# A decoder step on one core: front steps in another order, twelve more gathers ahead of a fence, and the last 32 keys' scores as three float32r products

## The chip, the core and the metric

The kernel runs on one core of a Trainium2 chip, in one launch. A core has five engines that run side by side, each with a queue of its own in fixed order: TensorE (PE in the profile; its weight loads are listed as PEld), VectorE (DVE), ScalarE (ACT), GpSimd (POOL) and SyncE (SP). SP, ScalarE and GpSimd also issue transfers, which share 16 DMA engines. The metric is the device time of one execution in microseconds (us).

## The reference, cut to what matters

512 prompt tokens and 8 x 4 sample tokens (544 in all) of width 1024 pass one layer. The first half mixes tokens: a projection to six parts, retention over chunks of 128 tokens in four heads, a causal convolution of width 31 with a norm, an output projection and a norm. The second half picks experts: 8 heads find 16 of 16384 experts for each token from two lists of 128 keys.

```python
q = (xb @ w_query).reshape(PEER_BLOCK, PEER_HEADS, PEER_DQ)
s1 = jnp.einsum('phd,hkd->phk', q1, sub_keys_1)
...
idx = e1 * N_KEYS + e2
gate = jax.nn.softmax(sv.astype(jnp.float32), axis=-1)
u = jnp.take(peer_u, idx, axis=0)
act = jax.nn.gelu(jnp.einsum('phkd,pd->phk', u, xb), approximate=False)
vv = jnp.take(peer_v, idx, axis=0)
return jnp.einsum('phk,phkd->pd', gate * act, vv)
```

The result is added to the scaled token and normalised again. All of it is float32.

## The kernel before, in words

The tokens are split into groups. Group 0 (prompt tokens 0 to 127) passes the first half alone, early. The rest (416 tokens: 32 samples, then three chunks of 128 prompt tokens) follows. Two ways lead through the experts:

- **Gathers** (`gather`, L567) for group 0, for group "s" (the samples; four lanes of 32, so 32 slots) and for group "b" (the first 128 of the later prompt tokens; 128 slots). A slot is one indirect transfer of 1 MB (L572, from GpSimd: one row of `u` and `v` for each of 128 tokens), a dot product on VectorE (L575), GELU and weight on ScalarE (L579, L580) and an addition to `acc` on VectorE (L585). The tiles come from pool `gp`, three buffers, with one more for every fourth slot (`gx` in the front for group 0, `gx2` for group "b").
- **The dense way** for the last 256 tokens (`ND`): all 128 x 128 experts are computed. For each of 128 table rows ("keys" `e` in the code), `scores_of` (L778) loads 512 KB of `u` and makes eight products of 128 x 128 by 256 columns in float32; GELU is taken and multiplied by the gates; `v_stage` (L914) loads 512 KB of `v` and adds four products of 512 columns to four PSUM banks `pB`, which hold two blocks of 128 tokens. The gate weights are built from comparisons (`build`, L855: ScalarE `off` and `A`, VectorE `M` and `B`, bf16 products on TensorE) for eight tokens at a time. `first_keys` (L888) builds keys 0 to 95, `last_keys` (L907) keys 96 to 127.

The keys lie in four groups (`EG`, `E0S`): 0 to 31 in `GW[0]`, 32 to 51 in `GW[1]`, 52 to 95 in `GW[2]`, 96 to 127 in `GW[3]`. Scores of groups 2 and 0 are made first (L830, L835), those of group 1 inside `first_keys`, and those of group 3 in `phases` (L923), one to each value row, once `last_keys` has ended. In `phases`, pool `gb` (group 0) is closed after its 32 value rows and `gd` (group 3) opened in its place.

The order of the work: each engine's queue follows a planner, which simulates the program at build time and takes the earliest instruction in program order that it holds to be ready. `behind` adds an order without a wait. One such order is the **fence** (L576): the dots of group "b" and those of group "s" from slot `FREE` (12) on come behind the last instruction of `first_keys` on VectorE. `run` (L597, L965) traces one value row and two gather slots in turn.

The front around the change (L690 to L750): the GLU projection, the convolution (`conv`), the value projection, `rope` for q and for k (L696, L697), retention of chunks 1 and 2 (L711, L712), the gate projection (`silu_gate`, L714), loads of `w_out` (L715), the sample columns' copies (L716, L718), the convolution's norm (`conv_norm`, L717), `gate_heads` for chunks 1 and 2, retention of chunk 3 (L741), `gate_heads` for it, and then the output projection and norm of four parts in turn (`mix_a`, `mix_b`, L743 to L750). Weights come through pool `wp`, four buffers of 1 MB, loaded from SP. Behind it (L797 to L804) the queries of the expert half are projected for two heads at a time over all 416 columns, and the top 16 are found (`retrieve`, L510).

At the end (L966 on) the two blocks of `pB` are normalised in turn into tiles of pool `uvp` and stored.

Of the kernel before, what the change touches and what calls it, by code (L numbers as in the profile page):

```python
# [8 lines left out]
F32 = mybir.dt.float32  # L9
F32R = mybir.dt.float32r  # L10
# [9 lines left out]
D = 1024  # L20
# [14 lines left out]
UV = 4  # L35
FREE = 12
# [57 lines left out]
def tile_step(ctx: ExitStack, tc: tile.TileContext, a, o):  # L94
# [50 lines left out]
    def load_win(blk):  # L145
        return load_w(a["w_in"], blk * 512)
# [631 lines left out]
    def scores_of(e):  # L778

        u = uvp.tile([128, D], F32, name="uv").rearrange("p (k e) -> p k e", k=8)  # L780
        nc.sync.dma_start(u, a["ut"][e])
        sp = pdn.tile([128, ND], F32, name="sp")
        for k in range(8):
            T.matmul(sp, u[:, k], x1T[:, k, NG2:], start=(k == 0), stop=(k == 7))  # L784
        return sp
# [45 lines left out]
    gbs = ExitStack()  # L831
    gb = gbs.enter_context(tc.tile_pool(name="gb", bufs=1, side="right", reuse_waits="tile"))
# [10 lines left out]
    gc = ctx.enter_context(tc.tile_pool(name="gc", bufs=1, reuse_waits="tile"))  # L843
# [70 lines left out]
    def v_stage(e):  # L914
        vt = uvp.tile([128, D], F32, name="uv")
        nc.sync.dma_start(vt, a["uv"][e * NK:(e + 1) * NK, D:])
        W = place(e)
        for b in range(2):
            for q in range(2):
                T.matmul(pB[b][q], W[:, b * 128:(b + 1) * 128], vt[:, q * 512:(q + 1) * 512],  # L920
                         start=False, stop=(e == NK - 1), skip_group_check=True)

    def phases():  # L923
        for e in range(EG[0]):
            v_stage(e)
            yield
        gbs.close()
        gd = ctx.enter_context(tc.tile_pool(name="gd", bufs=1, side="right", reuse_waits="tile"))
        GW[3] = gd.tile([128, EG[3], ND], F32, name="Gd")
        b = last_keys()  # L930
        more = iter(range(E0S[3], NK))
        for e in range(E0S[1], E0S[3]):
            v_stage(e)
            if next(b, "end") == "end":
                for _ in range(1):
                    k = next(more, None)
                    if k is not None:
                        s_stage(k)
            yield
        for e in range(E0S[3], NK):  # L940
            v_stage(e)
            yield

# [74 lines left out]
```

## Time and profile before

| what | value |
| --- | --- |
| device time, three runs | 1611.17, 1598.4, 1602.21 us; median 1602.21 |
| profiled execution, its own time | 1603.19 us |
| its span, first to last instruction | 1601.4 us |
| mean granted TensorE clock | 0.971 |
| busy PE, DVE, ACT, POOL | 1494.5, 1225.3, 604.3, 374.1 us |
| transfers | 503.75 MB, 315 GB/s over the span |

The page gives busy time in 40 slices as digits of a tenth. A line of a stretch of the span gives its bounds and length, then busy time and count of each engine, the granted TensorE clock, the DMA engines' busy share and GB/s. A waiting line reads: who waited, for whom, us in total, times, longest. A line of the timeline reads: start, length, engine, line of the kernel, operation, out<-in, shapes, count, and in brackets the idle time before it and what ended it. A busy TensorE is not TensorE at its peak, since matmuls overlap and their ends are modelled; starts of successive groups are safer.

### The profile page before, as it was taken

What the parts mean: (1) busy time and instruction counts of PE and PEld (TensorE: products, weight loads), DVE (VectorE), ACT (ScalarE), POOL (GpSimd) and SP (SyncE); (2) the same over time, 40 slices, a digit from 0 to 9 for tenths busy, and PEclk for the clock granted to TensorE, in tenths of its full rate; (3) what the DMA queues carried; (4) which work ended last, traced back from release to release, by engine and by line L of the source; (5) the groups of instructions that cost most, each with busy time, mean ns of one, the idle gap of its engine ahead of it and who ended that gap; (6) DMA issues with size and microseconds to landing.
All of it is one profiled execution on the core that took longest, in us unless ns stands there. A gap on an engine that the chain in (4) does not pass through costs nothing.

```text
span 1601.4 us, 20802 instructions
## 1 busy us (share of the span) xinstructions
PE 1494.5 (93%) x7014; PEld 1010.1 (63%) x7014; DVE 1225.3 (77%) x3158; ACT 604.3 (38%) x1687; POOL 374.1 (23%) x335
## 2 busy tenths in 40 slices
PE   6899999996979999999999997999999999999996
PEld 6788556564756667788788875444566655543332
DVE  3939989989865999999852788566777777766666
ACT  2235542254222323333623888413994111111111
POOL 1001423444321222321120000122223222222221
PEclk9899999998989999999999997999999999999998
DMA  9458778997698669997794321998999999999995
GB/s 355 180 195 347 253 280 301 354 364 253 253 383 321 260 250 340 345 340 271 251 413 157 108 86 57 398 402 332 385 365 380 423 424 424 424 423 424 424 424 211
DMA packets 99543, 503.75 MB, mean 315 GB/s; under 512 B 10183, under 2 KB 21191, under 8 KB 56549
## 3 DMA queue, kind: packets, MB, share of 16 engines
q0 software_dynamic: 42240, 305.12, 48.7%
q1 hardware_dynamic: 50749, 189.96, 31.3%
q10 hardware_dynamic: 6448, 7.36, 1.5%
q8 instruction: 55, 0.90, 0.2%
q14 instruction: 51, 0.42, 0.1%
HBM read 497.03 MB, written 5.80 MB: 314 GB/s over the span
## 4 chain that ended last, share of the span: by engine, by line
PE 32%; DMA 28%; DVE 24%; issue 8%; ACT 4%; POOL 2%; SPq 0%; DVEq 0%; POOLq 0%; ACTq 0%
DMA g<-in_uv_dram,Ib 17%; PE pB L920 10%; PE sp L784 9%; PE mm L198 7%; DMA g<-in_uv_dram,I 7%; DVE acc L585 6%; DVE g L575 4%; POOL g L572 2%; ACT off L862 2%; PE mm L875 2%; PE mm L308 2%; DMA g<-in_w_in_dram 2%; DMA uv<-in_uv_dram 1%; DVE iu L504 1%; DVE score L505 1%
## 5 line engine op out<-in xcount | busy, mean ns | idle before, releaser
L784 PE MATMUL sp<-x1T,uv 128*128 128x256 f32 x2048 | 464.7, 384 | 15.4 <-ACT Ga L830 9.4
L784 PEld LDWEIGHTS sp<-x1T,uv 128*128 128x128 f32 x2048 | 385.5, 191 | 89.5 <-issue 23.2
L585 DVE SCALAR_TENSOR_TENSOR acc<-g,wgt,acc 128x1024 f32<-128x1024 f32 x285 | 365.0, 1281 | 99.3 <-ACT wgt L580 98.1
L572 POOL DMA_INDIRECT g<-in_uv_dram,I x128 | 181.9, 1421 | 435.1 <-DVE acc L585 222.6
L579 ACT ACTIVATE act<-act 128x1 f32<-128x1 f32 x288 | 57.9, 201 | 592.4 <-DVE g L575 592.0
L575 DVE SCALAR_TENSOR_TENSOR g<-g,x1g 128x1024 f32<-128x1024 f32 x160 | 195.3, 1224 | 94.2 <-DMA g<-in_uv_dram,Ib 63.1
L572 POOL DMA_INDIRECT g<-in_uv_dram,Ib x128 | 133.5, 1043 | 517.9 <-DVE acc L585 318.5
L575 DVE SCALAR_TENSOR_TENSOR g<-g,x 128x1024 f32<-128x1024 f32 x128 | 155.6, 1217 | 31.9 <-DMA g<-in_uv_dram,I 31.8
L198 PE MATMUL mm<-x1T,w 128*128 128x384 f32 (+1 forms) x512 | 176.1, 500 | 0.2 <-ACT score L524 0.2
L920 PE MATMUL pB<-uv,Ga 128*128 128x512 f32 x352 | 162.1, 604 | 1.1 <-DMA uv<-in_uv_dram 0.8
L862 ACT ACTIVATE off<-row,e1T 128x128 bf16<-128x128 bf16 x512 | 157.8, 388 | 1.5 <-PE mm L875 0.4
L198 PEld LDWEIGHTS mm<-x1T,w 128*128 128x128 f32 x512 | 96.6, 190 | 71.4 <-issue 37.9
L920 PE MATMUL pB<-uv,Gd 128*128 128x512 f32 x256 | 117.2, 601 | 2.1 <-DMA uv<-in_uv_dram 1.0
L920 PE MATMUL pB<-uv,Gb 128*128 128x512 f32 x256 | 115.4, 604 | 2.9 <-DMA uv<-in_uv_dram 2.5
L920 PEld LDWEIGHTS pB<-uv,Ga 128*128 128x128 f32 x352 | 63.7, 189 | 83.7 <-issue 63.1
L920 PEld LDWEIGHTS pB<-uv,Gd 128*128 128x128 f32 x256 | 46.1, 189 | 73.3 <-issue 48.2
L875 PEld LDWEIGHTS <-A 128*128 128x128 bf16 x1536 | 64.6, 100 | 36.6 <-issue 32.0
L920 PEld LDWEIGHTS pB<-uv,Gb 128*128 128x128 f32 x256 | 48.1, 193 | 59.6 <-issue 54.3
L875 PE MATMUL mm<-B,A 128*128 128x96 bf16 (+1 forms) x1536 | 68.4, 197 | 13.3 <-DVE Gc L901 12.4
L864 ACT ACTIVATE A<-off 128x1024 bf16<-128x1024 bf16 x64 | 67.4, 1053 | 28.1 <-PE mm L875 27.7
L870 DVE TENSOR_TENSOR B<-M,gtT 128x768 bf16<-128x768 bf16 (+1 forms) x192 | 69.8, 419 | 9.8 <-PE mm L875 9.6
L920 PE MATMUL pB<-uv,Gc 128*128 128x512 f32 x160 | 72.3, 599 | 0.0
(279 smaller groups left out, 1706.3 us busy)
## 6 DMA issues: line engine op xcount, KB each, us to landing
uv<-in_ut_dram SPq DMA_DIRECT2D x128, 512.0 KB
uv<-in_uv_dram SPq DMA_DIRECT2D x128, 512.0 KB
w<-in_w_in_dram SPq DMA_DIRECT2D x18, 1024.0 KB
w<-in_w_query_dram SPq DMA_DIRECT2D x16, 1024.0 KB
w<-in_w_out_dram SPq DMA_DIRECT2D x7, 1024.0 KB
g<-in_uv_dram,I POOLq DMA_INDIRECT x128, 7.9
keys<-in_state_retention_dram ACTq DMA_DIRECT2D x4, 512.0 KB
out_dram<-keys SPq DMA_DIRECT2D x4, 512.0 KB
```

The costliest lines, as they stand in the source:

```text
L198: T.matmul(p[:, :n], w[m // 2][:, k, (m % 2) * 128:(m % 2 + 1) * 128], xT[:, k, c0:c0 + n], start=(k == 0), stop=(k == 7))
L308: mm = T.matmul(p[:n, q * 256:(q + 1) * 256], xT[:, k, c0:c0 + n], w[q][:, k, :], start=(k == 0), stop=(k == 7))
L572: G.indirect_dma_start(out=t, out_offset=None, in_=a["uv"], in_offset=bass.IndirectOffsetOnAxis(ap=idx[:, k:k + 1], axis=0))
L575: dot = V.scalar_tensor_tensor(t[:, :D], t[:, :D], 1.0, x1, op0=OP.mult, op1=OP.mult, accum_out=act[:, 0:1])
L579: S.activation(act[:, 1:2], act[:, 0:1], AF.Gelu)
L585: V.scalar_tensor_tensor(acc, v, wgt, acc, op0=OP.mult, op1=OP.add)
L784: T.matmul(sp, u[:, k], x1T[:, k, NG2:], start=(k == 0), stop=(k == 7))
L862: S.activation(off[:, t], row, AF.Abs, bias=e1T[:, t1 + t:t1 + t + 1])
L864: S.activation(A, off, AF.Relu, bias=1.0, scale=-1.0)
L870: V.tensor_tensor(B[:, q], M, pairs_of(gtT[:, q], t1).to_broadcast([128, TB // 2, ne, 2]), op=OP.mult)
L875: T.matmul(pt[:, t % nt], A[:, t - t1], B[:, q, (t - t1) // 2, :, t % 2], start=(q == 0), stop=(q == 2))
L920: T.matmul(pB[b][q], W[:, b * 128:(b + 1) * 128], vt[:, q * 512:(q + 1) * 512], start=False, stop=(e == NK - 1), skip_group_check=True)
```

## The change

- The front's order: gate projection and its sample copy ahead of `rope`; the weights of k and the first half of `w_out` loaded ahead of k's `rope`, the second half behind it; the sample copy of `y` and `conv_norm` ahead of the retention; chunks 1, 2 and 3 of the retention in a row; `gate_heads` of chunks 2 and 3 behind `mix_a` of the samples and chunk 1.
- The first two heads' query projection is made in two ranges of columns, 0 to 287 and 288 to 415.
- `FREE` goes from 12 to 24.
- The last 32 keys' scores: the 256 dense tokens are split once into a float32r copy and its rest (`xs`); each `u` row is split the same way by ScalarE and VectorE (`s_ready`), one step ahead of its use; a score is three float32r products, rest x copy, copy x rest and copy x copy, accumulated. Rest x rest is left out. The scores stand beside value rows 53 to 84.
- Memory: group 3 takes group 0's tile, `gb` stays open, group 1's pool closes at key 52 and makes room for the splits, and `gx2` lies on the right side.
- The last four value rows are loaded first, then multiplied for block 0 and then for block 1; the final tiles come from `gp`.

```diff
-FREE = 12
+FREE = 24
...
     vs += [project_v(w, xT, 128 * c, 128) for c in range(3)]
+    silu_gate(load_win(3), xT, n - NS, [(0, n - NS, gT[:, :, r])], False)
+    S.activation(gT[:, :, s_], gS, AF.Copy)
     rope(load_win(0), 0, xT, n - NS, 160, [(0, n - NS, qT)])
-    rope(load_win(1), 1, xT, n - NS, 160, [(0, n - NS, kT)])
-    wg = load_win(3)
+    wk_ = load_win(1)
+    wo = load_w(a["w_out"], 0)
+    rope(wk_, 1, xT, n - NS, 160, [(0, n - NS, kT)])
+    wo += load_w(a["w_out"], 512)
+    S.activation(y[:, :, s_], yS, AF.Copy)
+    conv_norm(y, n)
...
     retain(2)
-    banks[:] = [ps]
-    silu_gate(wg, xT, n - NS, [(0, n - NS, gT[:, :, r])], False)
-    wo = load_w(a["w_out"], 0) + load_w(a["w_out"], 512)
-    S.activation(y[:, :, s_], yS, AF.Copy)
-    conv_norm(y, n)
-    S.activation(gT[:, :, s_], gS, AF.Copy)
+    retain(3)
...
     gate_heads(ons[1], C, gT, NS)
-    gate_heads(ons[2], C, gT, NS + C)
-    retain(3)
-    gate_heads(ons[3], C, gT, NS + 2 * C)
     mix_a(0, NS, None)
     mix_a(NS, C, 0)
+    gate_heads(ons[2], C, gT, NS + C)
+    gate_heads(ons[3], C, gT, NS + 2 * C)
...
-    def scores_of(e):
+    xs, us = [], {}
+
+    def s_ready(e):
 
         u = uvp.tile([128, D], F32, name="uv").rearrange("p (k e) -> p k e", k=8)
         nc.sync.dma_start(u, a["ut"][e])
-        sp = pdn.tile([128, ND], F32, name="sp")
+        if not xs:
+            us[e] = ((u, x1T[:, :, NG2:]),)
+            return
+        uh, ul = xs[2].tile([128, 8, 128], F32R, name="uh"), xs[2].tile([128, 8, 128], F32R, name="ul")
+        S.activation(uh, u, AF.Copy)
+        V.tensor_sub(ul, u, uh.bitcast(F32))
+        us[e] = ((ul, xs[0]), (uh, xs[1]), (uh, xs[0]))
+
+    def scores_of(e):
+
+        if e not in us:
+            s_ready(e)
+        sp, terms = pdn.tile([128, ND], F32, name="sp"), us.pop(e)
         for k in range(8):
-            T.matmul(sp, u[:, k], x1T[:, k, NG2:], start=(k == 0), stop=(k == 7))
+            for j, (u, x) in enumerate(terms):
+                T.matmul(sp, u[:, k], x[:, k], start=(k == 0 and j == 0), stop=(k == 7 and j == len(terms) - 1))
...
-        for m in range(4):
-            S.activation(qs[:, h0 * 2 + m], project(w, m, x1T, 0, n), AF.Copy)
+        for c0, c1 in ((0, n - C), (n - C, n)) if h0 == 0 else ((0, n),):
+            for m in range(4):
+                S.activation(qs[:, h0 * 2 + m, c0:c1], project(w, m, x1T, c0, c1 - c0), AF.Copy)
...
-        gbs.close()
-        gd = ctx.enter_context(tc.tile_pool(name="gd", bufs=1, side="right", reuse_waits="tile"))
-        GW[3] = gd.tile([128, EG[3], ND], F32, name="Gd")
+        GW[3] = GW[0]
         b = last_keys()
-        more = iter(range(E0S[3], NK))
         for e in range(E0S[1], E0S[3]):
+            if e == 52:
+                gcs.close()
+                xsp = ctx.enter_context(tc.tile_pool(name="xsp", bufs=1, reuse_waits="tile"))
+                xs.extend(xsp.tile([128, 8, ND], F32R, name=n) for n in ("xh", "xl"))
+                S.activation(xs[0], x1T[:, :, NG2:], AF.Copy)
+                V.tensor_sub(xs[1], x1T[:, :, NG2:], xs[0].bitcast(F32))
+                xs.append(ctx.enter_context(tc.tile_pool(name="usp", bufs=2, reuse_waits="tile")))
+            if xs and E0S[3] + e - 52 < NK:
+                s_ready(E0S[3] + e - 52)
             v_stage(e)
-            if next(b, "end") == "end":
-                for _ in range(1):
-                    k = next(more, None)
-                    if k is not None:
-                        s_stage(k)
+            next(b, None)
+            k = E0S[3] + e - 52 - 1
+            if E0S[3] <= k < NK:
+                s_stage(k)
             yield
-        for e in range(E0S[3], NK):
+        for e in range(E0S[3], NK - UV):
             v_stage(e)
             yield
+        ends = [(e, v_row(e)) for e in range(NK - UV, NK)]
+        for b in range(2):
+            for e, vt in ends:
+                v_products(e, vt, b)
+                yield
...
-    gx2.append(ctx.enter_context(tc.tile_pool(name="gx2", bufs=1, reuse_waits="tile")))
+    gx2.append(ctx.enter_context(tc.tile_pool(name="gx2", bufs=1, side="right", reuse_waits="tile")))
     run((phases(), 1), (fetched(), 2))
     for b in range(2):
-        t = uvp.tile([128, D], F32, name="uv")
+        t = gp.tile([128, 2 * D], F32, name="g")[:, :D]
```

`v_row` and `v_products` are the two halves of the old `v_stage`: the load, and the two products of one block.

More of the change, by code (lines that the diff above doesn't have):

```diff
@@ L830, in tile_step @@
         S.activation(place(e), scores_of(e), AF.Gelu)
-    gbs = ExitStack()
-    gb = gbs.enter_context(tc.tile_pool(name="gb", bufs=1, side="right", reuse_waits="tile"))
+    gb = ctx.enter_context(tc.tile_pool(name="gb", bufs=1, side="right", reuse_waits="tile"))
     GW[0] = gb.tile([128, EG[0], ND], F32, name="Gb")
@@ L842, in tile_step @@
     dw_ = ctx.enter_context(tc.tile_pool(name="dw_", bufs=4, reuse_waits="tile"))
-    gc = ctx.enter_context(tc.tile_pool(name="gc", bufs=1, reuse_waits="tile"))
+    gcs = ExitStack()
+    gc = gcs.enter_context(tc.tile_pool(name="gc", bufs=1, reuse_waits="tile"))
     pacc = ctx.enter_context(tc.tile_pool(name="pacc", bufs=1, space=PSUM, reuse_waits="tile"))
@@ L912, in last_keys, with v_row, v_products, v_stage @@
                 yield
-    def v_stage(e):
+    def v_row(e):
         vt = uvp.tile([128, D], F32, name="uv")
         nc.sync.dma_start(vt, a["uv"][e * NK:(e + 1) * NK, D:])
+        return vt
+    def v_products(e, vt, b):
         W = place(e)
+        for q in range(2):
+            T.matmul(pB[b][q], W[:, b * 128:(b + 1) * 128], vt[:, q * 512:(q + 1) * 512],
+                     start=False, stop=(e == NK - 1), skip_group_check=True)
+    def v_stage(e):
+        vt = v_row(e)
         for b in range(2):
-            for q in range(2):
-                T.matmul(pB[b][q], W[:, b * 128:(b + 1) * 128], vt[:, q * 512:(q + 1) * 512],
-                         start=False, stop=(e == NK - 1), skip_group_check=True)
+            v_products(e, vt, b)
     def phases():
@@ L926, in phases @@
             yield
[L927 to L929 removed]
+        GW[3] = GW[0]
         b = last_keys()
[L931 removed]
         for e in range(E0S[1], E0S[3]):
[L933 to L938 removed]
+            if e == 52:
[7 more added lines that the diff above has]
+                s_ready(E0S[3] + e - 52)
+            v_stage(e)
+            next(b, None)
+            k = E0S[3] + e - 52 - 1
+            if E0S[3] <= k < NK:
+                s_stage(k)
             yield
[L940 removed]
+        for e in range(E0S[3], NK - UV):
             v_stage(e)
             yield
+        ends = [(e, v_row(e)) for e in range(NK - UV, NK)]
+        for b in range(2):
+            for e, vt in ends:
+                v_products(e, vt, b)
+                yield
     def fetched():
```

## The prediction

> **What bounds the kernel now.** I read the page first (the span in 40 slices), then stretches of the span by engine, then who waits for whom, then single instructions.
>
> ```profile
> span 1601.4 us, 20802 instructions
> ```
> ```profile
> PE   6899999996979999999999997999999999999996
> ...
> DVE  3939989989865999999852788566777777766666
> ...
> DMA  9458778997698669997794321998999999999995
> GB/s 355 180 195 347 253 280 301 354 364 253 253 383 321 260 250 340 345 340 271 251 413 157 108 86 57 398 402 332 385 365 380 423 424 424 424 423 424 424 424 211
> ```
>
> Each digit is a slice of 40 us. TensorE is near full nearly everywhere. The transfers have a hole from 840 to 1000 us (157 down to 57 GB/s) and a flat 424 from 1280 on. The same by stretches, in the columns busy PE, PEld, DVE, ACT, POOL, clock, DMA share, GB/s:
>
> ```profile
> 834.00:858.00 24.00, 24.00 (x113) 21.13 (x112) 0.38 (x1) 2.68 (x7) 0.94 (x1) 1.00 0.69 263
> 858.00:943.00 85.00, 80.29 (x704) 71.17 (x703) 61.63 (x232) 65.61 (x188) 0.00 (x0) 0.98 0.33 106
> ...
> 1000.00:1240.00 240.00, 238.88 (x1344) 128.24 (x1343) 167.78 (x299) 137.36 (x403) 65.82 (x56) 1.00 0.96 377
> 1240.00:1400.00 160.00, 157.72 (x524) 95.88 (x524) 115.48 (x151) 29.50 (x108) 41.10 (x44) 1.00 1.02 424
> 1400.00:1560.00 160.00, 158.00 (x353) 63.16 (x352) 108.97 (x131) 22.11 (x88) 40.06 (x43) 1.00 1.02 424
> ```
>
> So up to 1240 TensorE is the limit, and from 1240 on TensorE (158 of 160) and the transfers are full together. To see which of the two gives the pace there, I count rows. First the value products (L920, eight instructions a key), then the scores (L784, sixteen a key), then the gathers that GpSimd issues (L572), in the same stretches:
>
> ```profile
> 1240.00:1400.00 160.00, 79.09 (x172) 30.69 (x172) 1.00 1.02 424
> 1400.00:1560.00 160.00, 154.36 (x337) 60.21 (x336) 1.00 1.02 424
> ```
> ```profile
> 1000.00:1240.00 240.00, 32.89 (x144) 26.87 (x144) 1.00 0.96 377
> 1240.00:1400.00 160.00, 81.06 (x352) 65.19 (x352) 1.00 1.02 424
> 1400.00:1560.00 160.00, 3.69 (x16) 2.96 (x16) 1.00 1.02 424
> ```
> ```profile
> 1240.00:1400.00 160.00, 41.10 (x44) 1.00 1.02 424
> 1400.00:1560.00 160.00, 40.06 (x43) 1.00 1.02 424
> ```
>
> Table rows: 172/8 + 352/16 = 43.5 in the first stretch, 337/8 + 1 = 43.1 in the second; gathers 44 and 43. One row of 512 KB for one gather of 1 MB, every 3.7 us, whatever TensorE does with the row. What TensorE needs for a row:
>
> ```profile
> 1223.89 7.07 PE L784 MATMUL sp<-x1T,uv 128*128 128x256 f32 x32
> 1230.79 3.60 PE L920 MATMUL pB<-uv,Ga 128*128 128x512 f32 x8
> ```
>
> Two score rows take 1230.79 - 1223.89 = 6.90, so 3.45 us a row; a value row of 8 x 512 columns is as much work, 3.45. TensorE is thus 93% used (3.45 of 3.7), and the pace of the last 345 us is that of the shared transfers. The Trainium skill, DMA: Bandwidth & Descriptors, section Queues, rings and completion order, says that an engine goes round its queues packet by packet; the trace's 43 to 43 agrees with it. By that rule a faster score product gains nothing while gathers are queued: that is rival 2 below, 1586.
>
> **The front.** The two long waits of TensorE between 350 and 470 us, and instructions around them:
>
> ```profile
> PE mm L339 <- ACT on L332: 14.2, 2, 12.6
> ```
> ```profile
> 466.11 1.09 PE L486 MATMUL mm<-cst,xr 128*128 128x128 f32 x4 [11.24 <-DVE xr L455]
> ```
> ```profile
> 375.16 2.61 ACT L300 ACTIVATE blk<-blk,cols 128x416 f32<-128x416 f32 x4
> ```
> ```profile
> 379.29 0.64 PE L364 MATMUL mm<-v,sc 128*128 128x128 f32 x2
> ...
> 384.62 0.94 PE L374 MATMUL mm<-v,ktok 128*128 128x128 f32 x6
> ```
> ```profile
> 455.48 1.06 ACT L487 ACTIVATE x1T<-mm 128x512 f32<-128x512 f32 x2
> ```
>
> The 12.6 us stand before the transposes of chunk 2's head output, with chunk 3's retention (from 379.29 to 384.62 and on, some 5 us) queued behind. The change puts that retention ahead of the gating, so it falls into the hole: -5, and -1 because the products behind the pause ran slowly (0.64 for two of 128 columns). The rest of the hole stays, as the output projection needs the normalised convolution, which ScalarE ends at 377.8. The gate projection and w_out's loads move forward on TensorE and SP; their products and bytes stay the same, and SP only waits for the same four weight buffers in another order (0). On ScalarE two copies of sample columns move, and on GpSimd chunk 3's norm steps pass some gathers (0 each; no one waits for these gathers here). The 11.2 us stand before the last chunk's transposes, while the first 288 columns were ready at 456.5: the split query projection can run there, 466.1 - 456.5 = 9.6 us, for eight shorter groups of products in place of four (0). That makes 15.6. VectorE, full from 520 to 760 (all nines), will pass on only part: I take **-12**. Ends: -27 (both waits and the 3 us between), +5 if gathers that stand ahead on VectorE and GpSimd delay the moved chains.
>
> **The fence.** VectorE's longest wait between 834 and 992 us, and two free gathers before it:
>
> ```profile
> DVE Gb L899 <- ACT Gb L835: 24.4, 1, 24.4
> ```
> ```profile
> 827.31 1.23 DVE L575 SCALAR_TENSOR_TENSOR g<-g,x1g 128x1024 f32<-128x1024 f32 x1 [0.84 <-DMA g<-in_uv_dram,Is]
> 828.46 0.08 DVE L575 DVE_READ_ACCUMULATOR g<-g,x1g 128x1 f32 x1
> 829.14 1.29 DVE L585 SCALAR_TENSOR_TENSOR acc<-g,wgt,acc 128x1024 f32<-128x1024 f32 x1 [0.60 <-ACT wgt L580]
> ...
> 831.26 1.22 DVE L575 SCALAR_TENSOR_TENSOR g<-g,x1g 128x1024 f32<-128x1024 f32 x1 [0.84 <-DMA g<-in_uv_dram,Is]
> ```
>
> A gather takes 831.26 - 827.31 = 3.95 us, of it 2.5 on VectorE. Twelve more are 30 us of VectorE and 12.6 MB. Of the 24.4 us, 12 go to the earlier front; three gathers fit there. Nine fall between the token blocks from 858 to 943, where VectorE idles 85 - 61.6 = 23.4 us and 9 x 2.5 = 22.5 are asked. Behind each dot stand the next block's factors, for which TensorE waits: I take half a microsecond each, **+5**. Ends: 0 (nothing goes away here) and +15 (each waits 1.7 us for its landing). In return 12 x 3.7 = 44 us of gathers leave the last stretch.
>
> **The scores of the last 32 keys.** How many instructions a product has now:
>
> ```profile
> L784 PE MATMUL sp<-x1T,uv 128*128 128x256 f32 x2048 | 464.7, 384 | 15.4 <-ACT Ga L830 9.4
> ...
> L875 PE MATMUL mm<-B,A 128*128 128x96 bf16 (+1 forms) x1536 | 68.4, 197 | 13.3 <-DVE Gc L901 12.4
> ```
> ```profile
> 858.00:943.00 85.00, 22.61 (x432) 21.21 (x432) 0.98 0.33 106
> ```
>
> 128 keys x 8 products are 2048 float32 instructions, two a product, 3.45/16 = 0.216 us each. The bf16 products (32 blocks x 24 and 16 x 48) have one each: 22.61/432 = 0.052 us for 96 columns. No float32r product is in the trace. Lower end: a float32 pass, taken as half an instruction, 0.108, so 24 x 0.108 = 2.6 us a key. Upper end: as dear as float32, 24 x 0.431 = 10.3. Nearest is bf16, the other type that is rounded before use: 0.052 x 256/96 = 0.139 at most, 3.3 with each weight load in it. I take 2.7. The Trainium skill, FP8 and Floating Point Precision, TensorE Precision Notes, gives true float32 four passes and a reduced one that cuts to 22 bits; one pass would be the lower end, 2.6 us. That saves 32 x 0.75 = 24 us of TensorE, but a step of two rows needs 6.15 us of it and gets its rows in 7.4.
>
> The split costs a copy and a subtraction a key. The nearest rows of that size:
>
> ```profile
> 790.76 1.13 ACT L583 ACTIVATE acc<-g,wgt 128x1024 f32<-128x1024 f32 x1
> ```
> ```profile
> 1589.99 1.22 DVE L455 TENSOR_TENSOR yt<-yt,lnb 128x1024 f32<-128x1024 f32 x1
> ```
>
> ScalarE (29.5 of 160 busy) hides 1.13. VectorE gets 1.22 x 22 = 27 us more in the first stretch: 115.5 + 27 = 142 of 160, while its gathers also wait:
>
> ```profile
> DVE g L575 <- DMA g<-in_uv_dram,Ib: 56.0, 91, 1.6
> DVE acc L585 <- ACT wgt L580: 46.4, 90, 0.6
> ```
>
> 142 + 44 x 0.6 = 168 does not fit into 160 unless subtractions fill those waits. So gathers slow by some 5% and leave their bytes to rows: 3.55 in place of 3.7 us for 64 rows, -8 to -10. Without that (strict one to one) only two things are left: rows at 3.45 once the gathers have ended, 44 us earlier, 12 rows x 0.25 = -3, and the end of the stretch up to 1240, where today nine keys' scores (144 instructions) stand beside the last build and get cheaper or move behind it, -4. I take **-16** for the rows in all. Ends: -3, and -28 (the lesser of 12.6 MB at 424 GB/s, 29.7, and TensorE's 24 with the 4). The token split once is 2 x 1.13 and 2 x 1.22 beside 3.45 us of value products (0; 2 if they wait). The moved pools ask for no wait that was not there; the gather's fourth buffer only comes free sooner.
>
> **The end.** The last value products, and the last addition:
>
> ```profile
> 1568.33 18.19 PE L920 MATMUL pB<-uv,Gd 128*128 128x512 f32 x40 [1.01 <-DMA uv<-in_uv_dram]
> ...
> 1594.66 1.29 DVE L455 TENSOR_TENSOR uv<-uv,lnb 128x512 f32<-128x512 f32 x2
> ```
>
> From 1586.5 to 1595.9 are 9.4 us, in which the gathers' result (1589.99 above) and block 0 stand between block 1's steps on VectorE. With block 0 finished four half rows (4 x 1.73 = 6.9 us) earlier and the gathers ended before, four of the 1.2 us steps are gone from there; they fill waits in part, so **-2.5** (0 to -4).
>
> **Sum.** -12 + 5 - 16 - 2.5 = -25.5: span 1575.9. The profiled execution took 1603.19, 1.0 over the median, so 1577.7 by its own time and **1577** against the median of 1602.21.
>
> **The rivals.** (1) VectorE slows the gathers until both sides end together: the rows bring the whole -28. 1602 - 12 + 5 - 28 - 2.5 = 1565. For it: 168 against 160. Against it: 43 to 43 also where VectorE is 68% used. (2) The sharing stays one to one, as both stretches show it, and VectorE's subtractions fill its waits: rows -3 - 4 = -7, so 1602 - 12 + 5 - 7 - 2.5 = 1586. (3) The front's gain is eaten by VectorE, and the twelve gathers hold up the blocks or are not placed there, so that only part of the 44 us leaves the end: 0 + 12 - 12 - 2.5, 1600. For it: the blocks follow one another on VectorE, whose order is fixed. (4) Slower: a float32r product runs two passes or is paced by its weight load, 24 x 0.216 = 5.2 us a key. A step then needs 8.65 us, more than the 7.4 of its rows, 32 x 1.25 = 40 us on the path, less some 8 from rows that follow faster: 1602 - 12 + 5 + 32 - 2.5 = 1625. It decides from 3.95 us a key (7.4 - 3.45). Against it: bf16's single instruction. For it: 24 weight loads where there were 16.
>
> **How the numbers follow.** Forecast 0.32 (own range 1564 to 1588), rival 1 0.20, rival 2 0.18, rival 3 0.17, rival 4 0.10, 0.03 elsewhere. The range from 1551 to 1606 takes in rivals 1 to 3 with most of their ends and leaves out rival 4. About 1% (16 us) is what a measurement of this kernel tells from no change: faster are 0.31 of the forecast, rival 1, half of rival 2 and a little of rival 3, 0.63; within 1% the other half of rival 2 and most of rival 3, 0.24; slower rival 4 and its neighbours, 0.13.
>
> **What would show it.** Front: no wait of 11 us before L486, and the first top-16 before 500. Fence: 24 gathers of the small group before the first blocks' end, the hole's GB/s above 157, the stretch from 858 to 992 no more than 5 us longer. Scores: 24 instructions a key at 0.11, TensorE idling in the steps of two rows, rows closer than 3.7 us while gathers run, the last gather 30 to 45 us before the last value product. Wrong would be: a key's score over 3.95 us, a subtraction waiting for its row with gathers behind it, or gathers and rows still ending together.

## The result, and the profile after

The changed kernel takes 1647.16 us (median of 4 runs, 1645.65 to 1650.28); the kernel before takes 1601.16 us beside it (4 runs). The ratio is 1.027, 95% interval 1.024 to 1.030: 46 us slower, where 25 us faster was predicted. The profiled execution took 1650.28 us, span 1648.2. Its page, as 40 slices of 41 us:

```profile
span 1648.2 us, 21484 instructions
...
PE   7899899987959999999999989989978888889997
...
DVE  4939999898757999899668897667787777766631
...
PEclk9899999998979999999999988999989989899999
DMA  9469779987797779894998317899989999999962
GB/s 363 157 213 355 254 254 326 366 315 252 264 402 294 279 283 334 331 340 155 367 406 319 109 52 296 314 424 361 355 310 391 360 364 397 356 364 401 423 220 100
```

Three things differ from before. The hole of the transfers around 900 us is narrower, though not shallower (slice 22 now has 319 GB/s, where 157 stood; the lowest has 52, before 57). The flat 424 from 1280 us on is gone: 356 to 401 until 1520, with TensorE at 8 and its granted clock at 8 in places. And the last two slices have 220 and 100 GB/s: rows alone, without gathers. The same stretches as in the prediction, busy PE, PEld, DVE, ACT, POOL, clock, DMA share, GB/s:

```profile
1000.00:1240.00 240.00, 221.33 (x1262) 110.78 (x1261) 170.52 (x301) 144.14 (x407) 68.56 (x56) 0.96 0.93 356
1240.00:1400.00 160.00, 134.52 (x638) 94.69 (x637) 120.50 (x152) 44.09 (x115) 59.82 (x38) 0.94 0.97 377
1400.00:1560.00 160.00, 146.09 (x466) 79.75 (x467) 111.70 (x137) 30.19 (x96) 51.63 (x40) 0.94 0.98 384
```

Up to 1240 TensorE idles 19 us where it idled 1, and behind that neither TensorE nor the transfers are full any more. Rows and gathers from the value products (L938, eight a key), the scores (L799, 24 a key) and the gathers (L572), first up to 1240, then in the 240 us from there, in which all the split scores but three lie:

```profile
1000.00:1240.00 240.00, 195.42 (x426) 78.79 (x424) 0.96 0.93 356
...
1240.00:1480.00 240.00, 101.98 (x224) 41.38 (x224) 0.91 0.96 371
```
```profile
1000.00:1240.00 240.00, 11.20 (x68) 10.36 (x69) 0.96 0.93 356
...
1240.00:1480.00 240.00, 111.94 (x702) 102.42 (x701) 0.91 0.96 371
```
```profile
1240.00:1480.00 240.00, 88.57 (x56) 0.91 0.96 371
```

Up to 1240 that is 426/8 + 68/24 = 56.1 rows, where before had 432/8 + 144/16 = 63. In the next 240 us there are 28 + 29.25 = 57.25 rows and 56 gathers. The kernel before, value products, scores and gathers in the same 240 us:

```profile
1240.00:1480.00 240.00, 154.28 (x335) 60.08 (x335) 1.00 1.02 424
```
```profile
1240.00:1480.00 240.00, 84.76 (x368) 68.15 (x368) 1.00 1.02 424
```
```profile
1240.00:1480.00 240.00, 61.58 (x65) 1.00 1.02 424
```

335/8 + 368/16 = 64.9 rows and 65 gathers: rows and gathers slowed together, from 3.7 to 4.2 us. 6.9 and 7.6 rows are missing, and as rows run alone at the end, 14.5 rows of 3.45 us are 50 us: the last value products end at 1636.4 where they ended at 1586.5.

What waits there, in the waits of TensorE and of VectorE from 1240 to 1480 (us in total, times, longest):

```profile
PE sp L799 <- DVE ul L789: 36.5, 13, 3.2
PE pB L938 <- DMA uv<-in_uv_dram: 2.6, 2, 1.7
```
```profile
DVE Gb L902 <- ACT W L899: 30.8, 20, 3.2
DVE acc L585 <- ACT wgt L580: 21.9, 38, 0.6
DVE ul L789 <- ACT uh L788: 5.0, 5, 2.3
DVE g L575 <- DMA g<-in_uv_dram,Ib: 1.8, 1, 1.8
```

TensorE waits for subtractions, hardly for rows (2.6 us). VectorE hardly waits for gathers (1.8 us, before 39.1); it waits for the gelu of scores. So the waits form a ring: score, gelu, copy, subtraction, next score. One turn of it, in order of time:

```profile
1259.05 0.28 PE L799 MATMUL sp<-xh,uh 128*128 128x256 f32 x1
1259.37 0.38 ACT L899 ACTIVATE W<-sp 128x256 f32<-128x256 f32 x1 [4.80 <-PE sp L799]
1259.65 1.05 ACT L788 ACTIVATE uh<-uv 128x1024 fp32r<-128x1024 f32 x1
1259.79 0.42 DVE L902 TENSOR_TENSOR Gb<-Gb,W 128x256 f32<-128x256 f32 x1 [2.76 <-ACT W L899]
1260.73 1.23 DVE L789 TENSOR_TENSOR ul<-uv,uh 128x1024 fp32r<-128x1024 f32 x1 [0.52 <-ACT uh L788]
...
1262.01 0.58 PE L799 MATMUL sp<-xh,ul 128*128 128x256 f32 x1 [2.68 <-DVE ul L789]
1262.39 0.41 PE L799 MATMUL sp<-xl,uh 128*128 128x256 f32 x1
```

The score ends; only then ScalarE takes its gelu (ScalarE had idled for 4.80 us before it), and only behind that the copy of the next row (for rows to land ScalarE waits 0.9 us in all the 240). VectorE waits 2.76 us for that gelu, then for the copy, subtracts, and the next score starts. The program asks for the split a step ahead; in the queues it stands behind the score before. And behind the pause the products come every 0.21 us instead of 0.12, for some 2.8 us.

### The profile page after: what moved, and what is told of

It reads as the page before. It is cut to its first block, busy times and chain, and to the rows that moved or that the text cites. A ratio compares the mean times of both kernels' runs of the same rounds, so it can differ in the third digit from the quotient of the medians.

```text
span 1648.2 us, 21484 instructions
## 1 busy us (share of the span) xinstructions
PE 1489.6 (90%) x7334; PEld 1035.6 (63%) x7334; DVE 1259.5 (76%) x3191; ACT 637.3 (39%) x1724; POOL 417.6 (25%) x335
## 4 chain that ended last, share of the span: by engine, by line
PE 29%; DVE 23%; DMA 18%; issue 17%; POOL 9%; ACT 3%; POOLq 0%; SPq 0%; DVEq 0%; ACTq 0%
PE sp L799 11%; POOL g L572 8%; PE pB L938 8%; DMA g<-in_uv_dram,Ib 8%; DMA g<-in_uv_dram,I 7%; DVE acc L585 5%; PE mm L198 5%; DVE g L575 4%; PE mm L891 2%; DMA g<-in_w_in_dram 2%; DVE score L505 1%; DVE iu L507 1%; DVE iu L504 1%; DMA uv<-in_uv_dram 1%; PE mm L308 1%
## 5 line engine op out<-in xcount | busy, mean ns | idle before, releaser
L799 PE MATMUL sp<-x1T,uv 128*128 128x256 f32 x1536 | 348.2, 384 | 10.9 <-ACT Ga L846 6.6
L799 PEld LDWEIGHTS sp<-x1T,uv 128*128 128x128 f32 x1536 | 290.6, 192 | 53.7 <-ACT Ga L846 8.4
L572 POOL DMA_INDIRECT g<-in_uv_dram,Ib x128 | 176.4, 1378 | 453.6 <-DVE acc L585 322.0
L572 POOL DMA_INDIRECT g<-in_uv_dram,I x128 | 173.8, 1358 | 433.5 <-DVE acc L585 237.8
L938 PE MATMUL pB<-uv,Gb 128*128 128x512 f32 x512 | 231.4, 603 | 2.4 <-DMA uv<-in_uv_dram 1.4
L198 PE MATMUL mm<-x1T,w 128*128 128x384 f32 (+3 forms) x576 | 175.8, 463 | 0.7 <-ACT on L428 0.7
L938 PEld LDWEIGHTS pB<-uv,Gb 128*128 128x128 f32 x512 | 94.8, 191 | 129.0 <-issue 104.4
L938 PE MATMUL pB<-uv,Ga 128*128 128x512 f32 x352 | 160.4, 603 | 2.6 <-DMA uv<-in_uv_dram 2.6
L799 PE MATMUL sp<-xh,ul 128*128 128x256 f32 x256 | 88.1, 344 | 40.6 <-DVE ul L789 40.6
L938 PEld LDWEIGHTS pB<-uv,Ga 128*128 128x128 f32 x352 | 65.7, 195 | 74.3 <-issue 69.1
L799 PEld LDWEIGHTS sp<-xh,ul 128*128 128x128 f32 x256 | 57.4, 224 | 54.9 <-DVE ul L789 51.6
L799 PE MATMUL sp<-xh,uh 128*128 128x256 f32 x256 | 81.9, 320 | 0.0
L799 PE MATMUL sp<-xl,uh 128*128 128x256 f32 x256 | 80.4, 314 | 0.0
```

The lines of the kernel that those rows point to most:

```text
L198: T.matmul(p[:, :n], w[m // 2][:, k, (m % 2) * 128:(m % 2 + 1) * 128], xT[:, k, c0:c0 + n], start=(k == 0), stop=(k == 7))
L572: G.indirect_dma_start(out=t, out_offset=None, in_=a["uv"], in_offset=bass.IndirectOffsetOnAxis(ap=idx[:, k:k + 1], axis=0))
L799: T.matmul(sp, u[:, k], x[:, k], start=(k == 0 and j == 0), stop=(k == 7 and j == len(terms) - 1))
```

## The experiments

Theory: the steps with a score are slow because TensorE's score hangs on the subtraction in VectorE's fixed order. Rivals: rows are delivered late (delivery); VectorE simply has too much to do (load); the order of gelu and copy alone (order). Medians are compared with runs of the kernel before on the same chip (1601 to 1605 us), so the ratio is what counts.

### Float32 scores in the changed kernel

```diff
-                xs.extend(xsp.tile([128, 8, ND], F32R, name=n) for n in ("xh", "xl"))
...
-            if xs and E0S[3] + e - 52 < NK:
+            if E0S[1] + 20 <= e and E0S[3] + e - 52 < NK:
```

> The changed kernel with the last 32 keys' scores as plain float32 products again: no split, no subtraction, everything else of the change kept (front, fence at 24, loads one step ahead, tail). Theory (ring): in the steps with a score VectorE is taken all the time: from 1240 to 1480 us two gathers, a subtraction and a multiplication by the gelu fill 8.2 us a step of value row and score, and TensorE waits 36.5 us for subtractions. Without the subtraction VectorE needs two gathers and 0.42, some 6.5 us, the step falls back to the 7.4 us of the transfers, TensorE's waits for VectorE are gone: 29 steps x 0.8 = 23 us and some 5 of the slow products behind pauses, 1615 to 1622 us. Rival (delivery): the steps are long because rows are issued too late or get too small a share of the transfers; then a step stays at 8.2 us and the time within 5 us of 1647, with waits for uv in place of waits for ul. Float32 costs 0.57 us more of TensorE a key, which hides in either case.

1614.99 us, ratio 1.006 (1.003 to 1.008). The stretch from 1240 is back at the transfers' pace, with 299/8 + 432/16 = 64.4 rows and 64 gathers:

```profile
1240.00:1480.00 240.00, 235.50 (x731) 133.49 (x730) 170.46 (x221) 42.71 (x157) 72.17 (x64) 1.00 1.02 422
```

Delivery falls: the same loads in the same order arrive in time. By the medians 32 us of the loss hang on the split.

### The subtraction on GpSimd

```diff
-        V.tensor_sub(ul, u, uh.bitcast(F32))
+        G.tensor_sub(ul, u, uh.bitcast(F32))
```

> The changed kernel with the subtraction of the table rows (1.22 us on VectorE) on GpSimd; all else kept. Ring theory: VectorE then needs two gathers (2 x 2.58 and the waits for the weights) and 0.42 a step, 6.5 us, so the step falls to about 7.4 us, limited by the transfers, if GpSimd's subtraction takes less than some 3 us beside its two gather issues of 1 to 1.7 us: 1615 to 1625 us. Rival (delivery): step stays at 8.2, about 1645. Rival (order alone: ScalarE takes the gelu of a key ahead of the next row's copy, so split and score follow one another in a chain whichever engine subtracts): copy, subtraction and score stay in line, step 7.9 to 8.2, 1637 to 1647.

1705.61 us, ratio 1.064 (1.060 to 1.067): no theory expected it. The costliest groups on VectorE and the subtraction on GpSimd from 1240 to 1480 (busy us, mean ns):

```profile
L585 DVE SCALAR_TENSOR_TENSOR acc<-g,wgt,acc 128x1024 f32<-128x1024 f32 x46 | 110.5, 2402 | 17.9 <-ACT wgt L580 17.9
```
```profile
L789 POOL TENSOR_TENSOR ul<-uv,uh 128x1024 fp32r<-128x1024 f32 x24 | 56.5, 2356 | 3.2 <-ACT uh L788 2.8
```

It takes 2.36 us there, and the additions to `acc`, 1.28 us otherwise, take 2.40 in the mean. So VectorE is as busy as before (175.5 us of the 240, 177.1 in the changed kernel) with 46 gathers in place of 56, and the run tells nothing between the theories. The Trainium skill, SBUF — State Buffer, section Who interferes with whom, describes a port pair that VectorE and GpSimd share as an exclusive lock, and says that a VectorE instruction with two SBUF inputs contends with a GpSimd instruction that reads SBUF; the single additions, from 1.28 to 3.69 us, agree with that.

### The split really a step ahead

```diff
+        if e + 1 in nxt:
+            behind(first, nxt[e + 1][0])
+            behind(then, nxt[e + 1][1])
```

`first` and `then` are the gelu of a key and its multiplication, `nxt` the copy and subtraction of a row.

> The changed kernel with an order only: the gelu of a key stands behind the copy of the next row on ScalarE, and its multiplication behind the next row's subtraction on VectorE, so that the split really is a step ahead in the queues. VectorE keeps all its work. Order theory: the 30.9 us that VectorE waits for the gelu and the 5.0 that it waits for the copy (1240 to 1480 us, 29 steps) go away; a step needs 7.5 us of VectorE instead of 8.3, near the 7.4 of the transfers: 1615 to 1625 us, TensorE's waits for the subtraction below 10 us. Load theory (VectorE simply has too much to do, the waits on the gelu only stand where it would have waited for a gather anyway): the waits move to the gathers' landing, step 8.0 or more, 1638 to 1647 us.

1632.43 us, ratio 1.016 (1.011 to 1.021), between the two. VectorE's wait for the gelu fell to 7.7 us, the stretch has 259/8 + 742/24 = 63.3 rows and 61 gathers, and TensorE still waits 25.3 us for subtractions. By the medians the order is about a third of the loss.

### The front alone, and the front undone

The first is the kernel before with the front's part of the diff, the second the changed kernel without it.

```diff
+    silu_gate(load_win(3), xT, n - NS, [(0, n - NS, gT[:, :, r])], False)
...
+    conv_norm(y, n)
...
+    retain(3)
...
+        for c0, c1 in ((0, n - C), (n - C, n)) if h0 == 0 else ((0, n),):
```

> The kernel before with the front's part of the change alone (order of gate projection, k's rope, convolution norm, retention, gate_heads, and the split query projection). Theory: the last chunk's norm stands behind a gather's dot product that waits 3.9 us for its landing, and the query products cannot start before the second chunk's columns are copied, so the first top 16 comes 5 us later (505.9 before): 2 to 6 us slower than before, 1603 to 1608. Rival: the delay of 5 us in the changed kernel came from other parts that shift the planner's order; alone the front gains the 12 us predicted, about 1590.

> The changed kernel with the front as before (its order and the undivided query projection). The front alone cost 0.3% (0.1 to 0.6) on the kernel before. Theory: the front's delay passes through to the end, 1640 to 1644 us. Rival: VectorE's load behind it swallows the delay, 1646 to 1648.

Alone 1610.51 us, ratio 1.003 (1.001 to 1.006), some 5 us slower and a little more than expected. Undone 1637.0, ratio 1.023 (1.018 to 1.028): 10 us below the changed kernel by the medians, 7 by the ratios, whose intervals overlap. The marks agree: the first top 16 (its first product, queries by keys, L521) comes at 499.5 to 512.3 us, 506.4 in the mean, in nine profiles with the old front, and at 509.7 to 523.0, mean 515.2, in seven with the new. In the changed kernel the 12.6 us ahead of L339 shrank to 1.3, as predicted; the pause ahead of L486 grew. TensorE, and VectorE in front of it:

```profile
462.57 1.23 DVE L575 SCALAR_TENSOR_TENSOR g<-g,x 128x1024 f32<-128x1024 f32 x1 [3.85 <-DMA g<-in_uv_dram,I]
...
464.92 0.69 DVE L447 BATCH_NORM_STATS2 lst<-mm 128x6 f32<-128x512 f32 x1
...
468.70 0.69 DVE L447 BATCH_NORM_STATS2 lst<-mm 128x6 f32<-128x512 f32 x1
469.25 1.06 ACT L487 ACTIVATE x1T<-mm 128x512 f32<-128x512 f32 x2
...
475.95 1.08 PE L486 MATMUL mm<-cst,xr 128*128 128x128 f32 x4 [17.67 <-DVE xr L455]
```

The last chunk's statistics stand behind two gathers that wait for their data. The same hold ScalarE's copy of the second-last chunk's columns until 469.25, transposed at 457.24; so the first 288 columns of the query projection were ready only at 470.3, late in the pause, and as it stands behind the last chunk's transposes in TensorE's queue, it began at 480.27.

### The fence, and the share of rows and gathers

`fence24` is the kernel before with FREE = 24. `fence24_3buf` also leaves out the fourth gather buffer, `spare_half` uses it for 64 of the last 128 slots, `rows6` adds two row tiles in its stead:

```diff
-FREE = 12
+FREE = 24
...
-    gx2.append(ctx.enter_context(tc.tile_pool(name="gx2", bufs=1, reuse_waits="tile")))
...
+            if len(slots) == 128 and spare is not gx and k >= 64:
+                spare = None
...
+                    uv2.append(ctx.enter_context(tc.tile_pool(name="uv2", bufs=2, reuse_waits="tile")))
```

> The kernel before with FREE = 24 as its only edit. In the run with float32 scores the gathers ended some 48 us ahead of the rows, and up to there rows and gathers still went one to one (64.4 rows, 64 gathers in 240 us). Theory (one to one): twelve gathers leave the last stretch, the first blocks end 0 to 3 us later, and some 12 rows run at TensorE's 3.45 in place of 3.7 us once the gathers have ended: 0 to -4 us, 1597 to 1603. Rival (the transfers' bytes bound the end, so 12.6 MB less are 30 us less): 1572 to 1580.

> FREE = 24 on the kernel before and the fourth gather buffer (gx2) left out, so that every gather of the last group uses one of three. Theory (the share follows the bytes in flight): four row tiles of 0.5 MB stand against four gathers of 1 MB now, two to one in bytes, which is one to one in number; with three gathers rows get 40% of 424 GB/s, one in 3.1 us, more than TensorE's 3.45 asks. Some 90 rows run 0.25 us faster, and 79 gathers at 3.85 still end before them: -20 us, 1578 to 1585. Rival (one to one holds whatever the buffers, or three buffers starve the gathers and they end last): 1597 to 1610, gathers to the end or rows at 3.7 beside them.

> The kernel before with FREE = 24 and the fourth gather buffer used only for the first 64 of the last group's 128 slots. With four buffers throughout rows and gathers went one to one, rows ended at 1583 and gathers at about 1530; with three throughout rows went at TensorE's pace (69.5 in 240 us), gathers at 4.36 us each, rows ended at 1566 and gathers at about 1597. Theory (share follows the bytes in flight): half and half brings both ends near 1570 to 1575, end 1580 to 1586 us, 1.0 to 1.4% faster than before. Rival (the difference between the two runs is a shift of the whole execution and not the share): 1594 to 1600.

> The kernel before with FREE = 24 and two more row tiles (in the room that the last build leaves, so from the first score step on): six rows of 0.5 MB in flight against four gathers of 1 MB. Theory (share follows the bytes in flight): rows get 43% of 424 GB/s, one in 2.9 us, so TensorE's 3.45 is the limit of rows, and gathers keep the rest, 3.86 us each, and still end first: rows 0.25 us faster over some 78 rows, 1576 to 1584 us. Rival (rows are paced one to one by the queues, whatever is in flight): 1594 to 1600 as with FREE = 24 alone.

1596.97, 1606.8, 1587.12 and 1596.52 us; ratios 0.997 (0.995 to 1.000), 1.002 (1.000 to 1.004), 0.991 (0.988 to 0.995), 0.997 (0.995 to 0.999). `fence24` came as its theory said: with FREE = 24 the stretch from 1240 has 64.5 rows and 65 gathers, still one to one. With three buffers the value products, scores and gathers read:

```profile
1240.00:1480.00 240.00, 162.19 (x369) 70.22 (x370) 1.00 0.99 389
```
```profile
1240.00:1480.00 240.00, 84.45 (x374) 70.55 (x372) 1.00 0.99 389
```
```profile
1240.00:1480.00 240.00, 59.24 (x55) 1.00 0.99 389
```

369/8 + 374/16 = 69.5 rows, TensorE's own 3.45 us, and 55 gathers, which now end last. The expected 1578 to 1585 missed that: gathers took 4.36 us, not 3.85; the rival's starved gathers, 1597 to 1610, gave the time. With six row tiles it is 376/8 + 368/16 = 70 rows and 56 gathers, so the counts again moved as the tiles did, but the time is the rival's (1594 to 1600), not the expected 1576 to 1584. VectorE in that stretch, with six row tiles:

```profile
DVE Gd L886 <- ACT W L883: 55.2, 18, 6.1
DVE g L575 <- DMA g<-in_uv_dram,Ib: 9.9, 17, 1.1
```

With FREE = 24 alone these waits are 7.8 and 27.0 us, with three buffers 38.4 and 29.4. So with six row tiles the gathers were held mostly by VectorE's fixed order, in which their additions stand behind the multiplication of a score that isn't done, and not by late landings. That the one to one of before is no rule of the queues is shown, and it moved with what is held in flight; how much of the gathers' part is the transfers and how much VectorE's order is not separated. Half and half balances the ends: rows end at 1564.8, gathers at 1557.3, and the time is 1 us above the expected range.

### One product a key

```diff
-        us[e] = ((ul, xs[0]), (uh, xs[1]), (uh, xs[0]))
+        us[e] = ((uh, xs[0]),)
```

> The changed kernel with one float32r product a key, copy x copy, in place of three: the two products with the rests and the subtraction are left out, so the scores carry only the rounded parts. TensorE then needs about 1 us a key, VectorE no more than for plain float32. Theory (one to one): a step of value row and score stays at the 7.4 us of its two rows and two gathers, TensorE idles a third of it, and the time is that of the float32 scores, 1605 to 1617 us. Rival (TensorE's score is on the path in these steps): 2.4 us less a key, 32 keys, 77 us off the 1615 of the float32 scores: about 1540. Clock rival: pauses of TensorE slow the products behind them, 1620 or more.

1604.42 us, ratio 1.001 (0.999 to 1.003). A key needs eight products of 0.12 us where float32 needs 3.45 us, and the time is 11 us below float32's (1615), not 77. The stretch has 326/8 + 216/8 = 67.8 rows beside 63 gathers: a faster score is worth little while gathers are queued.

### The subtraction made, but not waited for

`split_first` with two products a key; rest x copy is left out, and nothing reads the subtraction's result.

```diff
-        us[e] = ((ul, xs[0]), (uh, xs[1]), (uh, xs[0]))
+        us[e] = ((uh, xs[1]), (uh, xs[0]))
```

> The run with the split held a step ahead, but the score uses only two products (copy x rest of the tokens, copy x copy): the subtraction of each table row is still made on VectorE, and no product reads it; the product rest x copy is left out. VectorE's load is that of split_first (1632 us). Dependence theory: rows no longer wait for VectorE, gathers alone bear the 1.22 us: rows run closer than the gathers (more than 66 rows in the 240 us from 1240, 58 to 62 gathers), 1605 to 1615 us. Load theory: rows and gathers stay together at about 63 and 61, 1625 to 1635 us.

1618.05 us, ratio 1.010 (1.007 to 1.013). VectorE carries the same load and is taken all the time (195.3 busy and 44 in waits, of 240), yet:

```profile
1240.00:1480.00 240.00, 197.84 (x733) 111.08 (x732) 195.32 (x247) 64.20 (x181) 102.24 (x64) 0.96 1.02 420
```

64 gathers, 301/8 + 432/16 = 64.6 rows, 420 GB/s. So the load alone does not slow the stretch. The time is 14 us below `split_first` (1632), though the intervals of the ratios overlap. It goes with TensorE's dependence on the subtraction, but the third product went too, and no run separates the two. The expected surplus of rows over gathers did not come, and rows do still wait, now for ScalarE's copy:

```profile
PE sp L798 <- ACT uh L788: 40.5, 26, 1.9
```

### What could be made of it

`best_f32r` is the changed kernel with the old front, the split held ahead, the spare buffer for 64 slots, and the last four rows held in the order block 0, block 1. `rows6_tail` adds that order to `rows6`. `spare72_tail` is the kernel before with FREE = 24, the spare for 72 slots and that order, written out:

```diff
+                    if last is not None:
+                        behind(mm, last)
+                    last = mm
```

> The changed kernel with the front as before, the split really one step ahead in the queues (order of gelu and multiplication behind the next row's copy and subtraction), the fourth gather buffer only for 64 of 128 slots, and the last rows held in the order of the blocks. Theory: front -10, order -15, share -5 to -10 on 1647: 1605 to 1620; VectorE still has two gathers, the subtraction and the multiplication in a step, so the float32r scores do not get below the float32 version of the same edits (1580 to 1586 expected of it). Rival (once the waits in line are gone and gathers take less, TensorE's 0.57 us a key comes through): 1570 to 1580.

> The same and the last four rows' products held in the order block 0, then block 1, by orders without a wait (in the changed kernel the planner put the four rows one after another again, so that the norms of the two blocks stood 1.7 us apart). Theory: block 0's norm starts 6.9 us ahead of the last product, only block 1's steps stand behind it: 1.5 to 3 us less than the run with six rows. Rival (block 1's own chain from its last product to the last addition is all that counts, 6.6 us in either order, and the last rows' landing now comes ahead of all products): no difference, or up to 2 us more.

> The kernel before with FREE = 24, the fourth gather buffer for 72 of the last group's 128 slots, and the last four rows held in the order of the blocks. With 64 slots and without the held order it was 1587 us, and the gathers' result was normalised between the two blocks' norms at the very end. Theory: gathers end some 5 us earlier, rows 1 us later, the norms no longer meet: 1582 to 1586 us. Rival: balance and end were already as good as they get: 1586 to 1590.

1599.13, 1594.71 and 1584.31 us; ratios 0.997 (0.995 to 0.999), 0.996 (0.994 to 0.998), 0.988 (0.985 to 0.991). The last is the fastest found, 1.2% below the kernel before, with float32 scores. The held order by itself is 1.8 us, which overlapping intervals don't settle. `best_f32r` came out below its expected 1605 to 1620 and far above the rival's 1570 to 1580; it beats the changed kernel by 2.9% and still loses to the float32 version: TensorE waits 13.9 us for subtractions from 1240 on, and up to 1240 it is busy 222.5 us of 240, where `spare_half` has 235.2.

## Why the prediction was wrong

**What bounds** was read rightly, and drawn out too far. Both limits were where I saw them. "Whatever TensorE does with the row" was not: the counts held while four row tiles stood against four gathers, and moved apart with three buffers and with six row tiles. The rule of the Trainium skill that I set beside it (DMA: Bandwidth & Descriptors, Queues, rings and completion order) goes round the queues that have work; it does not say how long each has. Rival 2, strict one to one, is what the float32 run did (64.4 rows, 64 gathers); the 1586 that went with it counted on 12 us from the front, which did not come.

**The rows** are the step that failed: "So gathers slow by some 5% and leave their bytes to rows: 3.55 in place of 3.7 us". The sum on VectorE, 168 of 160 us, named the right engine, though a load like it just fits in `sub_unused`, and I named the hitch ("unless subtractions fill those waits", and among the signs of error a subtraction with gathers behind it). But I charged it to the gathers alone. The rows of the scores pass through the same queue: TensorE's products hang on `ul`, so the delay came to both: TensorE waits 36.5 us for subtractions, and rows and gathers both went to some 4.2 us. The term, -16, became +42 to +47: of the span's +46.8 the front took 5 to 10, while the builds gave 2.2 and the end 2.8.

What hangs on which part can be read from the medians, and once more from the profiles behind the first top 16. Up to that mark the kernels with the same front run the same instructions in the same order, and single executions still reach it up to 13 us apart; behind it, one profile each, in us:

| kernel | first top 16 | span | from the mark to the end |
| --- | --- | --- | --- |
| before | 505.9 | 1601.4 | 1095.5 |
| changed | 510.8 | 1648.2 | 1137.4 |
| `split_first` | 523.0 | 1637.8 | 1114.8 |
| `sub_unused` | 518.3 | 1615.0 | 1096.7 |
| `f32_scores` | 518.6 | 1613.7 | 1095.1 |
| `one_product` | 510.2 | 1602.0 | 1091.8 |

With float32 scores the changed kernel takes as long behind the mark as the kernel before. So the split costs 32 us by the medians and 42 by these profiles. Of that 15 and 23 go with the order of gelu and split (`split_first`), 14 and 18 with the subtraction that TensorE waits for and the third product together (`sub_unused`).

**The scores' place.** I took -4 for the nine scores that stood beside the last build and denied a new wait: "The moved pools ask for no wait that was not there". They do: `xh` lies in the room of group 1, whose last value row had to pass first, and ScalarE, full with the build, made the first row copies at 1219. Those scores had been what TensorE did meanwhile. ScalarE's copy of the tokens, and the page's stretches behind it, in the changed kernel:

```profile
1199.52 1.91 ACT L957 ACTIVATE xh<-x1T 128x2048 fp32r<-128x2048 f32 x1
```
```profile
1200.00:1220.00 20.00, 12.05 (x136) 6.70 (x134) 16.96 (x30) 19.27 (x52) 5.43 (x5) 0.84 0.82 294
1220.00:1240.00 20.00, 16.94 (x84) 13.11 (x85) 17.28 (x21) 6.66 (x17) 8.01 (x6) 0.82 0.89 326
```

With float32 scores at the same place TensorE is busy 20.0 and 18.7 us of these. One product, with no row subtracted, leaves it at 11.5 and 17.3, so the copies suffice.

**The score's price** was nearly right: I took 2.7 us a key, and at full clock products come every 0.12 us, 24 in 2.9. Rival 4, the slower one, fell by its mechanism; the time went past its 1625 by another.

**The front**: -12 became +5 to +10, near the +5 that I gave as its upper end, and by the cause named there, gathers ahead on VectorE. Rival 3 (gain eaten) held for the front. The query projection's 9.6 us of cover was taken from a profile in which ScalarE's copies of the columns came at 455; moving the chains moved these too.

**The fence**: +5 for the builds became -2 to -6. From the first top 16 to the value products behind the first blocks it takes 486.3 us before and 485.5 with the front alone, 480.8 with the fence alone, 484.1 in the changed kernel. VectorE's wait of 24.4 us for the last gelu of group 0 is 1.8 in the changed kernel, filled by gathers, and the blocks did not wait for them. That 44 us of gathers less gain little is shown by `fence24`, -4 us where one to one gave 0 to -4.

**The end**: -2.5 came, by another cause. From the last product (1636.4) to the last addition's end (1643.0) are 6.6 us, before 9.4; but the planner put the last four rows one after another again, and block 0's statistics start 1.7 us ahead of block 1's:

```profile
1633.89 0.70 DVE L447 BATCH_NORM_STATS2 lst<-pB 128x6 f32<-128x512 f32 x1 [49.00 <-PE pB L938]
...
1635.61 0.70 DVE L447 BATCH_NORM_STATS2 lst<-pB 128x6 f32<-128x512 f32 x1
```

The gain is the gathers' result, which was out of the way 49 us earlier. With the fence alone the end is as short.

What stays open: how the 11 us between one product and float32 divide (in the profiles 8.4 of them lie ahead of the first top 16, where both kernels run the same instructions, and 3.3 behind it), and why gather issues on GpSimd take 1.6 us in the split runs (0.95 before); no run separated the latter, and GpSimd waits for buffers anyway.

## What to carry to other kernels

Work given to a second engine puts that engine's queue into the first one's path: ask what stands ahead of the new instruction in its fixed order, and whether "a step ahead" in the program is a step ahead in every queue that it passes. When two streams share the transfers, what each holds in flight can move its share, as it did here, so balance their ends before making either consumer faster. Work that depends on nothing and stands beside a build is filler: whoever moves it has to name what fills its place.

## What the runs showed of the hardware that was not expected

- TensorE's products came at half their pace behind a pause of only 2.68 us: from 1262.01 every 0.21 us for 2.8 us, with a granted clock of 0.50, then every 0.12 at 1.00. The Trainium skill, TensorE: Matmul & The Clock Gate, Part 1, states at least one idle window of some 3.4 us for the clock to fall to half; this trace shows it behind a shorter pause, and the measurement decides.
- A float32r product of 128 x 128 by 256 costs 0.12 us in a row of its kind, with a weight load of 0.19 us listed for each and hidden: little over half of the 0.216 of one of float32's two instructions.
- An elementwise subtraction of 128 x 1024 on GpSimd takes 2.36 us (1.22 on VectorE), and additions of VectorE beside it up to 3.69 us instead of 1.28.
